# A hybrid encoder block: the last quarter of w_out in another order of token tiles, the first MLP stage in a written order, the second on shared tags

## The chip, the cores and the metric

The kernel runs on one core of one Trainium2 chip. The metric is the device time of one execution, in microseconds (us). Engines are named as the profile names them: PE is TensorE (matmuls), PEld its weight loads, DVE is VectorE, ACT is ScalarE, POOL is GpSimd, SP is the engine that issues most DMAs. ACT and POOL issue some DMAs too.

## The reference

One layer, one batch of 1024 tokens, model width 1024. Names as in the kernel:

```
h = RMSNorm(x)
[z | xBC | dt | q | k | v] = h @ W_in                 # 1024 -> 5664
ssd = gated norm of a bidirectional chunked scan (16 heads, 8 chunks of 128 tokens)
na  = neighbourhood attention on a 16 x 64 token grid, 16 heads of 64,
      QK-RMSNorm, window 8 x 16, relative-position bias
x = x + concat([ssd, na]) @ W_out                     # 2048 -> 1024
h = RMSNorm(x)
x = x + relu(h @ W1)^2 @ W2                           # 1024 -> 4096 -> 1024
```

Everything is float32. The kernel gets that accuracy out of matmuls on a rounded type: each operand is split into a high half (a rounded copy, made by ACT) and a low half (the rest, a subtraction by DVE or POOL), and a product takes three matmuls, high x high, high x low and low x high.

## The kernel before, in words

**Order of work.** After the input norm and the convolution (until 172 us in the trace) come the z, q, k, v pieces of W_in together with the scan (172 to 618), then the attention together with the first three quarters of w_out (618 to 892), the last quarter with the norm and the transposes for the MLP (892 to 974), the first MLP stage (first products from 942, alone from 975 to 1269) and the second (1272 to 1584).

**The planner.** From the pieces of W_in to the end of w_out the order of instructions on each engine comes from `Plan`: each task has an engine, an assumed cost in us, buffers that it reads and writes, and a due time; `order()` picks at each step the task that can start first (in steps of 0.35 us), the more urgent one where they tie. `run` emits the tasks in that order, inside `in_order()`, which ties each new instruction to the one before it on the same engine, so the framework's own scheduler can't move them. What is emitted outside `in_order()` the framework's scheduler orders by its own estimate of time.

**Attention.** Heads go in eight pairs; `due` puts a block of a head every 2.15 us, eight blocks a head. q and k lie in DRAM (`q_dr`, `k_dr`) as high and low halves, 64 rows for each head. `pair_loads` (L408 on) brings a pair: a q tile whose partitions 0 to 63 hold the high rows of one head and 64 to 127 the low rows (in the other order for the other head), with four DMAs of 256 KB; a k tile with the high rows in both halves, two DMAs of 512 KB for both heads at once; a tile `kl` with the low rows of k in one half and zeros in the other, two DMAs of 256 KB; and v, one DMA of 1024 KB. The scores are then two matmuls, q by k and q by kl (L1401, L1402). A w_out weight tile is loaded (L500), its high half made by ACT (L507), its low half by POOL (L510).

**The last quarter of w_out.** `groups` (L1772) is the order of 16 products, each a token tile t of 128 tokens by a half h of the columns, 12 matmuls. When both halves of a tile are added to x (`x2`, L1785), the tile is stored (`x2st`), squared and summed (L1791), its inverse root made by POOL in two instructions (`root`, L1794, L1795; the plan assumes 0.8 us), and it is normed by DVE (L1798), in place or, for tiles in `XB`, in a buffer `xn`.

**Seven products.** Both MLP stages multiply 2 x 2 blocks with seven products instead of eight (Winograd's form of Strassen's method), so sums and differences of blocks are needed: `difference` (L1770) makes those of the token tiles t and t+4, `turned` (L1758, L1762, L1763) transposes the results on PE and splits them into the operands `h1` to `h7`. Operands 1 and 2 need only tiles 0 to 3, operand 3 tiles 4 to 7, the others a pair (t, t+4). `ORD` = (1, 2, 6, 5, 7, 3, 4) is the order of the products. Products 1, 6, 7 and 4 collect in one set of PSUM tiles (X), 2 and then 5 and 3 in another (Y). So that PE has work while the last tiles are normed, three products of the first MLP stage are tasks of the plan: products 1 and 2 of block 0 and product 1 of block 1 (`block_product`).

**First MLP stage.** Eight blocks of 512 columns of W1 (`Block`). A product is 24 matmuls. `split` makes the weight operand, where needed from sums (`s1`, `s2`, L1583 to L1587), high half on ACT, low half on POOL (L369, L370); `sums` drains PSUM: copies on ACT (L1628), adds on DVE (L1633), relu and square on ACT (L1638, L1639), and the sums that are the operands of the second stage (L1646, L1648, L1650, L1654), stored to `act_dr` by SP (by POOL for the last block). In each block a product's split is emitted right ahead of the product, and the framework's scheduler places both.

**Second MLP stage.** Four parts, each with seven products of 48 matmuls; both operands are loaded and split anew: activations `ar` with ACT and DVE (`a_split`), weights with ACT and POOL, and weight differences on DVE (L1915, L1916, L1918, L1920). The results are added by DVE (L1945) to `acc`, which starts as x, loaded from DRAM (L1927), and is written out after the last part. This stage opens new SBUF pools and a new PSUM pool of its own, and is ordered by the framework's scheduler.

Of the kernel before, what the change touches and what calls it, by code (L numbers as in the profile page):

```python
# [10 lines left out]
F32 = mybir.dt.float32  # L11
# [219 lines left out]
def hymba_block(  # L231
# [64 lines left out]
    q_dr = dr.tile([2, 2, 4, P, T], F32, name="q_dr")  # L296
# [113 lines left out]
    def pair_loads(plan, p, after=()):  # L410
# [4 lines left out]
        qp = {(j, a): part(q) for j in range(2) for a in range(2)}  # L415
        kp = [part(k) for _ in range(2)]
        for j in range(2):
            for a in range(2):
                load_task(
                plan,  # L420
                    256,
                    partial(lambda j, a: q.t[a * HD : (a + 1) * HD, j].bitcast(F32), j, a),
                    partial(lambda j, a: q_dr[p // 4, a ^ j, p % 4, j * HD : (j + 1) * HD], j, a),
                    reads=after, writes=[qp[j, a]],
                    name="q",
                    since=-10.0 if p == 1 else -1e3,
                )
            load_task(
                plan,
                512,  # L430
                partial(lambda j: k.t[j * HD : (j + 1) * HD].bitcast(F32), j),
                partial(lambda j: k_dr[p // 4, 0, p % 4].rearrange("(h d) t -> d h t", h=2), j),
                reads=after, writes=[kp[j]],
                name="k",
                **free,
            )
        if p < 2:
            kls[p] = Buf(f"kl{i}"), []
            for j in range(2):
                half_, whole = part(kls[p][0]), kls[p][0]  # L440
                kls[p][1].append(half_)
                task("POOL", 1.0, partial(lambda j, b: nc.gpsimd.memset(b.t[HD * (1 - j) : HD * (2 - j), j].bitcast(F32), 0.0), j, whole), writes=[half_], name="kl0", **free)
        kl, klp = kls[i]
        for j in range(2):
            hp = slice(HD * j, HD * j + HD)
            load_task(plan, 256, partial(lambda hp, j: kl.t[hp, j].bitcast(F32), hp, j), partial(lambda hp: k_dr[p // 4, 1, p % 4, hp], hp), reads=after, writes=[klp[j]], name="kl", **free)
# [11 lines left out]
    def handed_on(plan, loaded):  # L458
# [3 lines left out]
        qp = {(j, a): part(q) for j in range(2) for a in range(2)}  # L462
# [58 lines left out]
    with ExitStack() as ph:  # L521
# [375 lines left out]
        def piece(j, b):  # L897
# [28 lines left out]
            to, w = (q_dr, 80) if kind(j) == "q" else (k_dr, 81)  # L926
# [6 lines left out]
            def turn():  # L933
                for i in range(4):
# [10 lines left out]
                    to[g, :, :, :, s].rearrange("a p f t -> f (a p) t"),  # L945
# [242 lines left out]
        def in_order():  # L1188
# [4 lines left out]
            for ins in traced[start:]:  # L1193
# [352 lines left out]
    with ExitStack() as ph:  # L1546
# [283 lines left out]
        for fb in range(8):  # L1830
# [3 lines left out]
            for i in ORD:  # L1834
                if i not in kb.w:
                    kb.split(i)
# [158 lines left out]
```

## Time and profile before

| | |
|---|---|
| median of 3 executions | 1585.77 us (1585.5 to 1588.29) |
| the profiled execution | 1589.21 us, of which its span is 1587.4 us |
| mean granted clock of PE | 0.992 |
| DVE, ACT, POOL busy | 1013.5, 720.9, 730.3 us (64%, 45%, 46% of the span) |
| DMA | 278.73 MB, 176 GB/s over the span |

The profile is of one execution. A row of its windows is: the stretch from:to in us, its length, then for PE, PEld, DVE, ACT and POOL the busy time with the number of instructions in brackets, then PE's granted clock (1.00 is full), the mean busy share of the 16 DMA engines, and GB/s. An instruction that lies in two windows counts in both. A row of the waits is: engine, tile and line that waited, what ended the wait, then us in total, times, longest. A row of the groups is: line, engine, operation, tiles, form, count, busy us, mean ns of one, idle time ahead of them and what ended it. A row of the timeline: start, us taken, what; of the chain: start, us, what; of the DMA issues: tiles, queue, count, KB each, median us from issue to landing. Matmuls overlap in the pipeline: one of 512 columns is recorded with some 0.39 us, while the next starts much sooner.

### The profile page before, as it was taken

The page shows a single profiled execution, that of the slowest core. Times are in us where ns is not written, and L with a number is a line of the kernel's source. Part 1 is how long each engine was busy: PE and PEld are TensorE (multiplying, and loading weights), DVE is VectorE, ACT ScalarE, POOL GpSimd, SP SyncE. Part 2 cuts the span into 40 slices and gives each one's busy share as a digit, 9 for nine tenths or more (in the row PEclk, how much of TensorE's full clock was granted, in tenths as well). Part 3 has the DMA queues.
Part 4 walks back from the last instruction along what each step waited for, and adds up shares of the span by engine and source line. Part 5 has one row for each costly group of instructions (what it writes and reads, how often), then busy time and mean ns, then how long its engine had stood idle before and what let it go on. Part 6 is the DMA issues. An engine that isn't in the chain of part 4 may idle for free. (4 is left out here: it accounts for less than half of the span.)

```text
span 1587.4 us, 20805 instructions
## 1 busy us (share of the span) xinstructions
PE 1548.1 (98%) x7462; PEld 1291.3 (81%) x7462; DVE 1013.5 (64%) x1414; ACT 720.9 (45%) x1187; POOL 730.3 (46%) x530
## 2 busy tenths in 40 slices
PE   7999999999999999999999998999999999999999
PEld 5788878888878888788888886888888778888887
DVE  3776444687688854567776475444444579787863
ACT  5444323444345435567686244554454444333330
POOL 2000066774779832233364353444444555555450
PEclk9999999999999999999999999999999989999999
DMA  8212398777777795978792422444443486443332
GB/s 225 54 40 70 89 311 262 231 238 248 230 209 214 225 278 172 257 208 227 193 238 94 159 94 93 174 158 146 151 155 120 159 306 251 159 161 131 107 106 80
DMA packets 184226, 278.73 MB, mean 176 GB/s; under 512 B 14819, under 2 KB 106043, under 8 KB 184123
## 3 DMA queue, kind: packets, MB, share of 16 engines
q1 hardware_dynamic: 133323, 233.88, 48.2%
q10 hardware_dynamic: 49792, 39.85, 7.6%
q0 software_dynamic: 1008, 3.67, 0.6%
q8 instruction: 59, 0.97, 0.3%
q14 instruction: 44, 0.36, 0.1%
HBM read 191.51 MB, written 89.18 MB: 177 GB/s over the span
## 5 line engine op out<-in xcount | busy, mean ns | idle before, releaser
L370 POOL TENSOR_TENSOR wl<-wraw,wh 128x1024 fp32r<-128x1024 f32 x113 | 308.7, 2743 | 305.5 <-ACT wh L369 305.5
L364 PE MATMUL pq<-wh,hTh 128*128 128x512 f32 x512 | 204.9, 400 | 2.3 <-DVE qn L931 1.7
L366 PE MATMUL pq<-wh,hTl 128*128 128x512 f32 x512 | 199.9, 390 | 0.0
L365 PE MATMUL pq<-wl,hTh 128*128 128x512 f32 x512 | 199.7, 390 | 0.1
L369 ACT ACTIVATE wh<-wraw 128x1024 fp32r<-128x1024 f32 x125 | 131.4, 1055 | 143.5 <-PE px L1221 40.1
L1221 PE MATMUL px<-wh,ahl 128*128 128x512 f32 x512 | 163.1, 395 | 4.6 <-ACT ahl L369 3.1
L1221 PE MATMUL px<-h,wh 128*128 128x512 f32 x512 | 160.1, 394 | 2.7 <-DVE cq L1633 2.7
L370 DVE TENSOR_TENSOR ahl<-ar,ahl 128x1024 fp32r<-128x1024 f32 x56 | 117.0, 2094 | 22.4 <-ACT ahl L369 21.5
L369 ACT ACTIVATE ahl<-ar 128x1024 fp32r<-128x1024 f32 x56 | 58.5, 1052 | 160.3 <-PE px L1221 80.6
L1221 PEld LDWEIGHTS px<-wh,ahl 128*128 128x128 f32 x512 | 97.6, 191 | 26.7 <-ACT ahl L369 3.6
L1221 PEld LDWEIGHTS px<-h,wh 128*128 128x128 f32 x512 | 96.6, 190 | 22.9 <-DVE cq L1633 3.1
L364 PEld LDWEIGHTS pq<-wh,hTh 128*128 128x128 f32 x512 | 96.2, 188 | 21.8 <-DVE qn L931 2.1
L366 PEld LDWEIGHTS pq<-wh,hTl 128*128 128x128 f32 x512 | 96.1, 188 | 20.8
L365 PEld LDWEIGHTS pq<-wl,hTh 128*128 128x128 f32 x512 | 96.3, 188 | 18.9 <-DVE wl L884 0.5
L1221 PE MATMUL px<-wl,ahl 128*128 128x512 f32 x256 | 101.3, 396 | 0.0
L1221 PE MATMUL px<-h,wl 128*128 128x512 f32 x256 | 100.4, 392 | 0.0
L1439 DVE TENSOR_TENSOR ptl<-ptp,pth 128x384 fp32r<-128x384 f32 (+1 forms) x128 | 65.4, 520 | 37.5 <-ACT pth L1441 36.5
L1405 DVE CUSTOM_DVE_ANT_0 pr<-psc,mb 128x384 f32<-128x384 f32 (+1 forms) x128 | 65.7, 520 | 26.6 <-PE psc L1402 23.5
L1417 ACT ACTIVATE pr<-pr,nmx 128x384 f32<-128x384 f32 (+1 forms) x128 | 74.6, 584 | 17.3 <-DVE nmx L1405 16.8
L1221 PE MATMUL pz<-h,wh 128*128 128x512 f32 x256 | 80.3, 395 | 0.8 <-DVE h L1763 0.8
L364 PE MATMUL po<-wh,yh 128*128 128x512 f32 x192 | 80.1, 417 | 0.2 <-DVE x L1327 0.2
L1221 PE MATMUL pz<-wh,ahl 128*128 128x512 f32 x256 | 80.1, 389 | 0.0
(332 smaller groups left out, 3743.4 us busy)
## 6 DMA issues: line engine op xcount, KB each, us to landing
ar<-act_dr SPq DMA_DIRECT2D x56, 512.0 KB, 4.4
act_dr<-cq SPq DMA_DIRECT2D x49, 512.0 KB, 3.0
wraw<-in_w_in_dram SPq DMA_DIRECT2D x44, 512.0 KB, 6.3
rb<-cum_dr SPq DMA_DIRECT2D x32, 512.0 KB, 6.1
wraw<-in_w_mlp_in_dram SPq DMA_DIRECT2D x32, 512.0 KB, 5.2
wraw<-in_w_mlp_out_dram SPq DMA_DIRECT2D x32, 512.0 KB, 5.6
q_dr<-hl ACTq DMA_DIRECT2D x16, 512.0 KB, 5.6
k_dr<-hl ACTq DMA_DIRECT2D x16, 512.0 KB, 3.6
```

What stands on the lines that cost most here:

```text
L364: nc.tensor.matmul(pt, lhsT=ah, rhs=bh, start=first, stop=False)
L365: nc.tensor.matmul(pt, lhsT=ah, rhs=bl, start=False, stop=False)
L366: return nc.tensor.matmul(pt, lhsT=al, rhs=bh, start=False, stop=last)
L369: nc.scalar.activation(hl[0], src, AF.Copy)
L370: eng.tensor_tensor(hl[1], src, hl[0].bitcast(F32), op=sub)
L1221: nc.tensor.matmul(pt, lhsT=a, rhs=b, start=f, stop=l, skip_group_check=True)
L1405: nc.vector.tensor_tensor_reduce(pr.t[:, 0:n], pt.t[:, 0:n], mb.t[:, o : o + n], scale=-1.0, scalar=3.0e38, op0=add, op1=ALU.min, accum_ou ...
L1417: nc.scalar.activation(pr.t[:, 0:n], pr.t[:, 0:n], AF.Exp, bias=nmx.t[:, b : b + 1], scale=-1.0, accum_out=den.t[:, hh, b : b + 1],)
L1439: nc.vector.tensor_tensor(lo[0], pv3, hi.bitcast(F32), op=sub)
```

## The change

1. **Rows of q and k.** `q_dr` changes its layout so that the high and low row of a feature lie next to each other, and the q tile holds them in alternating partitions: one DMA of 512 KB for each head over 128 partitions. k's high rows go to even and odd partitions, in four DMAs of 256 KB, each for one head; k's low rows to the even partitions. `kl` is zeroed whole. A head's scores now wait for that head's k only.
2. **Last quarter of w_out.** Another order of `groups`; tiles 3, 6 and 7 are normed into `xn` (5, 6 and 7 before); other due times; the root is planned with 1.2 us.
3. **First splits planned.** The sums of the weights of block 0 and the splits of its products 6 and 5 become tasks of the plan.
4. **First MLP stage in a written order.** Inside `in_order(skip=free_order)`, which leaves only SP to the scheduler, each step emits the split of the product after next, then its product, then its sums. Block 1 takes product 5 ahead of 6.
5. **Second MLP stage.** Its buffers are now tags of the first stage's pools (operand tiles h1 to h4 and h7, the b0 tiles that held operands 5 and 6, the weight rings, hq), and it keeps the same PSUM pool. `acc` is four tiles, two of them in the place of operand 4. The first loads and splits of part 0 are written between the products of block 7, and from there on each product of the second stage carries, between its four token tiles, the changes and splits for the product after next. All of that is in the written order.

```diff
-    q_dr = dr.tile([2, 2, 4, P, T], F32, name="q_dr")
+    q_dr = dr.tile([2, P, 2, 4, T], F32, name="q_dr")
...
+                partial(lambda j: q.t[:, j].bitcast(F32), j),
+                partial(lambda rows: q_dr[p // 4, rows, :, p % 4].rearrange("d a t -> (d a) t"), rows),
...
+            for a in range(2):
+                load_task(
+                    plan,
+                    256,
+                    partial(lambda j, a: k.t[a:P:2, j].bitcast(F32), j, a),
+                    partial(lambda rows: k_dr[p // 4, 0, p % 4, rows], rows),
+                    reads=after,
+                    writes=[kp[j]],
...
-                task("PE", 2 * (n / 2400 + 0.014), scores, reads=[qp[hh, 0], qp[hh, 1], *kp, klp[hh]], writes=[pt], due=due(b), name="psc")
+                task("PE", 2 * (n / 2400 + 0.014), scores, reads=[qp[hh], kp[hh], klp[hh]], writes=[pt], due=due(b), name="psc")
...
-        XB = [Buf("xn") if t > 4 else None for t in range(NT)]
+        XB = [Buf("xn") if t in (3, 6, 7) else None for t in range(NT)]
...
-        groups = [(0, 0), (1, 0), (2, 0), (0, 1), (1, 1), (2, 1), (4, 0), (4, 1)]
-        groups += [(3, 0), (3, 1), (5, 0), (5, 1), (6, 0), (6, 1), (7, 0), (7, 1)]
+        groups = [(0, 0), (4, 0), (1, 0), (0, 1), (4, 1), (1, 1)]
+        groups += [(t, h) for t in (5, 2, 6, 3, 7) for h in range(2)]
...
-            task("POOL", 0.8, root, reads=[ss], writes=[r0], name="r0")
+            task("POOL", 1.2, root, reads=[ss], writes=[r0], name="r0")
...
+            task("DVE", 1.23, partial(change, o, p, q, op), reads=read, writes=[b], since=52.0, name="mlps")
+        w6 = split_task(s2, Buf("w"), "POOL", due=68.0)
+        w5 = split_task(s1, Buf("w"), "POOL", due=74.0)
...
+        made = [(0, 1), (0, 2), (1, 1)]
+        row = [(fb, i) for fb in range(8) for i in ((1, 2, 5, 6, 7, 3, 4) if fb == 1 else ORD)]
+        left = [m for m in row if m not in made]
+        for fb, i in row[:49]:
+            kb = blocks[fb]
+            if i == 1:
+                kb.load("12", "21", "22")
+                kb.tiles()
+            with in_order(skip=free_order):
+                if (fb, i) in made:
+                    kb.to = kb.Y if i == 2 else kb.X
+                else:
+                    split_of(*left[left.index((fb, i)) + 2])
+                    kb.product(i)
+                kb.sums(i)
...
+        rings = {
+            "ahl": [over(hA, f"h{i}{n}") for i in (1, 2, 3) for n in range(2)],
+            "hl": [over(b0, t) for t in ("k", "v", "kl")] + [of_wp] * 3,
+            "raw": [over(arp, "wraw", F32), over(hq, "q", F32)],
+            "ar": [over(arp, "ar", F32), over(b0, "q", F32)],
+            "t": [over(hA, f"h7{n}", F32) for n in range(2)],
+        }
...
+            def ready(self, i, change=True):
+                for u in range(2):
+                    if change:
+                        self.change(i, u)
+                    yield
+                self.split_a(i)
+                yield
+                for u in range(2):
+                    self.split_w(i, u)
+                yield
...
+            kb.split(7)
+            kb.product(6)
+            o.split_a(1)
+            kb.sums(6)
+            o.load_a(2)
+            kb.split(3)
+            kb.product(5)
+            o.split_w(1, 0)
+            kb.sums(5)
+            o.load("12")
+            o.load("22")
+            kb.split(4)
+            kb.product(7)
+            o.split_w(1, 1)
+            o.split_w(2, 0)
+            kb.sums(7)
+            kb.product(3)
+            o.split_a(2)
+            o.split_w(2, 1)
+            kb.sums(3)
+            kb.product(4)
+            o.change(6, 0)
+            o.change(6, 1)
+            kb.sums(4)
+            load_acc(0)
+            row = [(o, i) for i in ORD] + [(p, i) for p in map(Part, range(1, 4)) for i in ORD]
+            for n, (o, i) in enumerate(row):
+                ahead = iter(row[n + 2][0].ready(row[n + 2][1], n > 0) if n + 2 < len(row) else ())
+                for _ in o.product(i):
+                    next(ahead, None)
+                if n == 1:
+                    begun = load_acc(1)
```

Here `split_w`, `split_a` and `change` are the weight split (ACT and POOL), the activation split (ACT and DVE) and the weight differences (DVE) of one product of part `o` of the second stage.

More of the change, by code (lines that the diff above doesn't have):

```diff
@@ L414, in pair_loads @@
         q, k, v = Buf(f"q{i}"), Buf(f"k{i}"), Buf(f"v{i}")
-        qp = {(j, a): part(q) for j in range(2) for a in range(2)}
-        kp = [part(k) for _ in range(2)]
+        qp, kp = ([part(b) for _ in range(2)] for b in (q, k))
         for j in range(2):
[L418 to L427, printed above, removed]
+            rows = slice(j * HD, (j + 1) * HD)
             load_task(
@@ L925, in piece @@
             qn, sq, rq, tp = Buf("qn"), Buf("sq"), Buf("rq"), Buf("tp")
-            to, w = (q_dr, 80) if kind(j) == "q" else (k_dr, 81)
+            w = 80 if kind(j) == "q" else 81
             col = pcol[:, w : w + 1]
@@ L1580, in split @@
                     self.load("12", "21", "22")
-                if i == 6:
+                if i in (5, 6) and "s1" not in a:
                     a["s1"], a["s2"] = raw_tile(), raw_tile()
@@ L1829, in hymba_block @@
         hq = ph.enter_context(tc.tile_pool(name="hq", bufs=1, reuse_waits="tile"))
-        for fb in range(8):
-            kb = (k0, k1)[fb] if fb < 2 else Block(fb)
-            kb.load("12", "21", "22")
-            kb.tiles()
-            for i in ORD:
-                if i not in kb.w:
-                    kb.split(i)
-                if not (i == 1 and fb < 2 or i == 2 and fb == 0):
-                    kb.product(i)
-                elif i == 1:
-                    kb.to = kb.X
-                else:
-                    kb.to = kb.Y
-                kb.sums(i)
@@ L1949, in hymba_block, with load_acc @@
                         )
+                    yield
+        def load_acc(h):
+            for n in range(2):
+                acc[2 * h + n] = t = over(*((hA, f"h4{n}"), (hq, "q"))[h], F32)("acc")
+                for m in range(2):
+                    last_ = nc.sync.dma_start(t[:, m], x2_dr[4 * h + 2 * n + m])
+            return last_
+        kb, o = blocks[7], Part(0)
+        kb.load("12", "21", "22")
+        kb.tiles()
+        o.load("11")
+        o.load_a(1)
+        o.load("21")
+        with in_order(skip=free_order):
+            kb.split(6)
+            kb.product(1)
+            kb.sums(1)
+            kb.split(5)
+            kb.product(2)
+            kb.sums(2)
+            kb.split(7)
[30 more added lines that the diff above has]
+                    begun = load_acc(1)
+                    tc_after = begun.ins
+                if i == 5 and o.fb < 3:
+                    row[n + 4][0].load_all(tc_after if o.fb == 0 else None)
+    b0s.close()
     arps.close()
```

225 lines of the change are left out of this document (119 added, 106 removed).

## The prediction

> **What bounds the kernel.** I read the page first, then the chain of waits that ended last, then TensorE's own waits.
>
> ```profile
> PE 1548.1 (98%) x7462; PEld 1291.3 (81%) x7462; DVE 1013.5 (64%) x1414; ACT 720.9 (45%) x1187; POOL 730.3 (46%) x530
> ```
>
> ```profile
> 1325.33 8.01 PE px L1221 x34
> 1333.33 10.88 PE pz L1221 x48
> ...
> 1572.69 10.89 PE px L1221 x48
> ```
>
> TensorE is busy 98% of the span of 1587.4 us, and the chain is TensorE alone from 1325 us on: 48 matmuls in 10.88 us, 0.2267 us each, without a hole. No edit changes the number or the shape of a matmul, so the change can only fill holes, and the page leaves 1587.4 - 1548.1 = 39 us of them, more where the clock was low. TensorE's waits say where they lie:
>
> ```profile
> PE po L365 <- POOL wl L510: 3.9, 2, 3.2
> PE pv L1369 <- ACT pth L1441: 3.3, 1, 3.3
> ...
> PE px L1221 <- DVE cq L1633: 2.7, 1, 2.7
> PE ptn L1758 <- POOL x L1770: 2.5, 1, 2.5
> PE ptn L1758 <- DVE h L1763: 2.3, 3, 1.3
> ```
>
> Three places: `po` and `pv` are the attention with the w_out quarters in it; `ptn` is the end of w_out's last quarter, with the norm and the transposes; `px` is the seam between the two MLP stages. The change touches all three.
>
> **Seam of the MLP stages.** The windows by 5 us:
>
> ```profile
> 1255.00:1260.00 5.00, 5.00 (x24) 4.14 (x23) 5.00 (x3) 1.06 (x1) 5.00 (x3) 1.00 0.69 257
> 1260.00:1265.00 5.00, 2.31 (x11) 1.61 (x10) 5.00 (x4) 0.20 (x1) 1.95 (x1) 1.00 0.00 0
> 1265.00:1270.00 5.00, 4.43 (x12) 3.14 (x12) 0.96 (x2) 5.00 (x6) 2.92 (x2) 0.66 0.01 3
> 1270.00:1275.00 5.00, 2.45 (x6) 1.97 (x7) 4.81 (x3) 5.00 (x7) 3.30 (x3) 0.68 0.90 311
> 1275.00:1280.00 5.00, 4.17 (x11) 2.77 (x10) 5.00 (x3) 3.18 (x4) 4.12 (x4) 0.50 0.99 378
> 1280.00:1285.00 5.00, 5.00 (x19) 3.99 (x18) 5.00 (x4) 0.00 (x0) 3.71 (x3) 0.80 1.03 415
> ```
>
> A full window shows 24 matmuls (first row). The next five show 59 instead of 120: 61 x 0.2267 = 13.8 us lost, part of it in waiting, part in the clock of 0.50 to 0.80 that follows the waiting. VectorE is full at the start of it, with this:
>
> ```profile
> 1259.62 3.42 DVE L1916 TENSOR_TENSOR wraw<-wraw 128x1024 f32<-128x1024 f32 x1
> 1262.96 1.21 DVE L1918 TENSOR_TENSOR wraw<-wraw 128x1024 f32<-128x1024 f32 x1
> 1264.09 0.67 DVE L1633 TENSOR_TENSOR cq<-cq,px 128x512 f32<-128x512 f32 x1
> ```
>
> Differences of the second stage's weights (L1916, L1918) stand ahead of the add (L1633) that frees the PSUM tile of block 7, and product 4 waits for that tile. The new code writes the order out: the add comes before the second stage's work, and product 1's operands are split during products 6, 5 and 7 of block 7. The cover, engine by engine, a product of block 7 being 24 x 0.2267 = 5.44 us:
>
> POOL, at 2.5 us a split (row L370 below), has at most three in one product (7.5 us) and then one in the next, 10 us in 10.9; it also issues block 7's seven stores, which the new splits are moved past:
>
> ```profile
> 1269.22 0.57 POOL L1619 DMA_DIRECT2D act_dr<-cq  x1
> ```
>
> 0.6 us each, 4 us in five products, so it still ends ahead of product 1. VectorE has, after product 3, three sums, four weight differences and the last sum, 8 x 1.21 = 9.7 us behind 2.8 us of relu and square (priced below), and reaches product 1's first add 7 us after that product began. That holds the adds to `acc`, not TensorE: product 1's PSUM is wanted again by product 6, 2 x 10.88 = 21.8 us after product 1 began. The new wait is that of the `acc` loads: their buffers are now operand 4's, so they can issue only when product 4 has read it. Queued behind them on SP are the next activation loads, on VectorE everything behind the first add. Four loads of 512 KB take 5 to 7 us at the 311 to 415 GB/s of the windows, inside the 21.8; uncovered they would cost those 5 to 7. In all -13.8, less 1.0 for a first product that starts ragged: **-12.8** (bounds -13.8 and -7). Within the second stage every operand is written two products ahead, and the chain has no hole there now: 0.
>
> **Last quarter of w_out.** First its last `po` matmul, then the windows behind it:
>
> ```profile
> 941.50 0.39 PE L366 MATMUL po<-wside,kl 128*128 128x512 f32 x1
> ```
>
> ```profile
> 950.00:975.00 25.00, 19.36 (x104) 15.25 (x103) 19.60 (x23) 11.15 (x19) 11.06 (x6) 0.93 0.15 46
> ```
>
> ```profile
> 975.00:980.00 5.00, 5.00 (x17) 3.90 (x15) 1.37 (x3) 2.21 (x4) 0.00 (x0) 0.68 0.87 297
> ```
>
> Idle 25 - 19.36 = 5.6; clock 0.07 x 19.36 + 0.32 x 5 = 3.0: 8.6 us. Tile t+4 is subtracted from tile t, and only then can four of the seven operands be transposed. Before, the pairs (0,4), (1,5), (2,6), (3,7) completed at steps four, six, seven and eight; now at two, four, six and eight, so one pair's differences are left at the end where two were bunched. That last chain (add, square, root, norm, four differences, transposes) has the three planned products as cover, 3 x 5.44 = 16.3 us. Against it: tile 3 is now seventh instead of fifth. It is multiplied one step (24 matmuls, 5.4 us) ahead of the last, and its own add, square, root, norm and transposes take longer than that, so operands 1 and 2, which the planned products read, can come after the last `po`; and three weight differences with two POOL splits are planned into a stretch where VectorE is busy 19.60 of 25. Bounds: -8.6, all hidden, and +2.7, half a step bare. I take **-5.5**, nearer the first, since TensorE's waits in this stretch are for differences (L1770) and what follows them.
>
> **Attention.** Rows of q and k are interleaved: a q load now fills 128 partitions where it filled 64, in two DMAs a pair instead of four, and k comes in four of 256 KB instead of two of 512. Bytes are the same. The windows, ScalarE's longest wait for a DMA, and the loads:
>
> ```profile
> 665.00:670.00 5.00, 4.49 (x25) 3.71 (x23) 2.96 (x9) 1.00 (x4) 2.07 (x3) 1.00 1.07 368
> 670.00:675.00 5.00, 1.78 (x7) 1.21 (x7) 0.00 (x0) 0.00 (x0) 2.61 (x2) 1.00 1.03 239
> 675.00:680.00 5.00, 2.15 (x8) 1.76 (x9) 2.24 (x5) 3.74 (x10) 2.37 (x1) 0.79 0.60 171
> ```
>
> ```profile
> ACT wh L507 <- DMA wraw<-in_w_out_dram: 10.3, 1, 10.3
> ```
>
> ```profile
> v<-v_dr SPq DMA_DIRECT2D x8, 1024.0 KB, 7.3
> q<-q_dr SPq DMA_DIRECT2D x32, 256.0 KB, 9.1
> k<-k_dr SPq DMA_DIRECT2D x16, 512.0 KB, 8.6
> ```
>
> One hole of 0.51 + 3.22 + 2.85 us, with 0.21 x 2.15 in the clock: 7.0 us. ScalarE stood 10.3 us for a w_out weight while the DMA engines were full (share 1.03 to 1.07). A q load has a quarter of v's bytes and lands later. If q, k and kl held the engines for less time, that weight would land sooner; but the planner gets other tasks and orders the whole stage anew. Bounds: -7.0, and +7.0 for one such hole elsewhere. I take **-3.0**, nearer to the q and v rows than to the reshuffle.
> [...]
>
> **First MLP stage in a written order.** Here nothing can be won:
>
> ```profile
> 1000.00:1025.00 25.00, 25.00 (x112) 20.72 (x111) 11.51 (x10) 12.50 (x17) 12.17 (x5) 1.00 0.52 189
> ```
>
> Splits are written two products ahead; the tightest is that of product 6 of the next block. VectorE, POOL and ScalarE from 1000 to 1250 us:
>
> ```profile
> L1650 DVE TENSOR_TENSOR cq<-cq 128x1024 f32<-128x1024 f32 x7 | 21.8, 3108 | 0.0
> ...
> L1633 DVE TENSOR_TENSOR cq<-cq,py 128x512 f32<-128x512 f32 x14 | 9.6, 685 | 24.9 <-ACT cq L1628 14.7 <-PE py L1221 10.2
> ...
> L1648 DVE TENSOR_TENSOR cq<-cq 128x1024 f32<-128x1024 f32 x7 | 8.5, 1215 | 0.0
> ```
>
> ```profile
> L370 POOL TENSOR_TENSOR wl<-wraw,wh 128x1024 fp32r<-128x1024 f32 x47 | 117.3, 2496 | 137.2 <-ACT wh L369 137.2
> ```
>
> ```profile
> L369 ACT ACTIVATE wh<-wraw 128x1024 fp32r<-128x1024 f32 x47 | 49.9, 1062 | 90.8 <-issue 30.1 <-PE pz L1221 25.5 <-PE px L1221 23.7
> ```
>
> After product 3: add, relu and square, 0.7 + 2 x 1.06 = 2.8; six VectorE sums in a row (three of product 3, one of product 4, two for the weight), 6 x 1.22 = 7.3; one POOL split in front of one of them, 2.5; then 1.06 and 2.5 for the split of product 6 itself: 16.2 us. Product 6 starts three products later, 16.3 us, and needs the low half at its third matmul, 0.45 on. Half a us of slack, with hand-overs between engines not counted, at six block changes: **+1.0**. Bounds 0 and +12, if one more POOL split comes in front and each block change is 2.0 us late.
> [...]
>
> **Sum.** -12.8 - 5.5 - 3.0 + 1.0 = -20.3. The profiled execution took 1589.2 (its span and 1.8 around it), so 1568.9; it lies 3.4 above the median of 1585.77, on whose scale that is **1565.5**.
>
> **Rivals.**
> A, the forecast: 1565.5, by its own unknowns 1558 to 1572. 0.60.
> B, the slow loads were the whole cause in the attention: -7.0 in place of -3.0, 1561.5. For it the q and v rows; against it that a weight also waits for a free buffer. 0.13.
> C, the new tile order doesn't do what it says: the last pair's chain ends as late as before, since tile 3 comes late and VectorE is nearly full. 5.5 back, 1571. 0.11.
> D, product 6 is late at each block change: 12 back, 1577.5; at 3 us each 18 back, 1583.5. For it the half us of slack; against it that POOL has one split to put in front, not two. 0.08.
> E, slower: two k loads now write alternate rows of one half tile. If the second is held until the first has landed, 8.6 to 9.1 us come twice in a row. Place: the start of each of the seven pairs loaded in the attention; price: that of the measured hole, 7.0 us. From three late pairs on (21 us) the gain is gone; at five it is 1565.5 + 35 = 1600. Against it: the plan gives a pair 16 x 2.15 = 34 us, and the next is loaded meanwhile. 0.08.
>
> **How the numbers follow.** A measurement of this kernel can tell about 0.2%, 3.2 us, from no change: 1582.6 to 1588.9 is the same. Faster: A, B, C and half of D, 0.88. Same: the other half of D, and E at three pairs, 0.06. Slower: the rest of E, 0.06. At its best the last quarter gives 3.1 more, the attention 4.0, the block changes 1.0 and the seam 1.0: 1556.4, the low end. The high end takes in C, and D at 12: 1580. Left out are E and the far half of D, 0.12.
>
> **What would show it.** Right: 24 matmuls in every 5 us through the seam at a clock of 1.00; under 4 us lost between the last `po` and the first stage's steady run; no ScalarE wait near 10 us for w_out, and q loads landing well under 9.1 us. Wrong: TensorE waiting for `wl` L370 at every block change, 38 us apart (D); for q or k at pair starts (E); or for the adds to `acc` at product 6 of the second stage.

## The result and the profile after

| | before | after |
|---|---|---|
| median | 1585.63 us (1583.2 to 1588.29, 4 runs) | 1559.13 us (1557.95 to 1562.73, 4 runs) |
| profiled execution | 1589.21 us, span 1587.4 | 1558.86 us, span 1557.1 |
| mean granted clock of PE | 0.992 | 1.000 |

The ratio is 0.9836, 95% interval 0.9814 to 0.9859: 26.5 us or 1.6% faster. The page after, first row:

```profile
PE 1535.2 (99%) x7462; PEld 1284.3 (82%) x7462; DVE 1000.1 (64%) x1414; ACT 725.8 (47%) x1187; POOL 709.6 (46%) x530
```

The same 7462 matmuls; TensorE's idle time went from 39 to 1557.1 - 1535.2 = 22 us.

**Seam.** Windows after, where block 7 ends and the second stage begins:

```profile
1240.00:1245.00 5.00, 5.00 (x24) 4.14 (x23) 3.68 (x2) 3.18 (x4) 5.00 (x3) 1.00 0.38 108
1245.00:1250.00 5.00, 5.00 (x24) 4.14 (x23) 2.78 (x4) 2.67 (x4) 3.31 (x2) 1.00 0.77 268
1250.00:1255.00 5.00, 5.00 (x24) 4.14 (x23) 4.93 (x5) 3.39 (x4) 2.16 (x4) 1.00 0.99 338
1255.00:1260.00 5.00, 5.00 (x24) 4.14 (x23) 4.97 (x6) 3.07 (x4) 0.66 (x2) 1.00 1.04 385
```

24 matmuls in each at full clock: the hole is gone. VectorE after, from its timeline, has the add (L1639) 15 us ahead of the differences (L1942), which stood in front of it before:

```profile
1237.45 0.69 DVE L1639 TENSOR_TENSOR cq<-cq,px 128x512 f32<-128x512 f32 x1 [2.04 <-PE px L1227]
1241.32 4.75 DVE L370 TENSOR_TENSOR ahl<-ar,ahl 128x1024 fp32r<-128x1024 f32 x2 [3.17 <-ACT ahl L369]
...
1253.02 1.22 DVE L1942 TENSOR_TENSOR wt<-wraw 128x1024 f32<-128x1024 f32 x1
```

**Last quarter of w_out.** Windows after, and TensorE's waits from 920 to 1000 us:

```profile
925.00:950.00 25.00, 22.50 (x129) 18.68 (x128) 22.91 (x29) 13.38 (x23) 13.65 (x9) 1.00 0.23 85
950.00:975.00 25.00, 25.00 (x120) 20.88 (x119) 7.51 (x12) 11.44 (x16) 9.58 (x4) 1.00 0.40 127
975.00:1000.00 25.00, 23.87 (x106) 19.43 (x105) 14.93 (x13) 15.21 (x18) 10.59 (x4) 1.00 0.51 188
```

```profile
PE px L1227 <- DVE h L1769: 2.5, 1, 2.5
PE pz L1227 <- POOL wl L370: 1.1, 1, 1.1
```

The waits for `ptn` have gone, and the clock stays at 1.00. Two holes remain, 2.5 us idle before the first product of the MLP and 1.1 us where block 0 passes into block 1.

**Attention.** The window of the hole, before and then after, and three kinds of load after:

```profile
665.00:690.00 25.00, 18.42 (x97) 15.77 (x96) 12.11 (x33) 10.78 (x30) 11.95 (x10) 0.93 0.89 245
```

```profile
665.00:690.00 25.00, 25.00 (x154) 22.43 (x153) 18.58 (x52) 17.25 (x46) 9.78 (x10) 1.00 0.85 285
```

```profile
k<-k_dr SPq DMA_DIRECT2D x32, 256.0 KB, 6.5
q<-q_dr SPq DMA_DIRECT2D x16, 512.0 KB, 6.2
wraw<-in_w_out_dram SPq DMA_DIRECT2D x16, 512.0 KB, 6.7
```

The hole is not there, a q load of twice the size lands in 6.2 us instead of 9.1, and ScalarE no longer waits for a w_out weight.

To compare stages, I use the time that TensorE lost in them, from each run's one trace: over the stage's matmuls, what each spacing from start to start exceeds the usual spacing of the same two shapes in that trace, summed; a low clock counts in it. The tail is the last quarter of w_out with what follows it up to 1000 us, the seam the place where the second MLP stage begins. All runs of this study:

| kernel | median us | span us | attention 600-900 | w_out tail 900-1000 | second stage from 1225 |
|---|---|---|---|---|---|
| before | 1585.6 | 1587.4 | 28.4 | 12.3 | 13.6 |
| place_only | 1580.1 | 1579.5 | 19.6 | 11.5 | 13.4 |
| rows_only | 1579.3 | 1578.3 | 18.5 | 11.7 | 14.2 |
| diffs_later | 1582.8 | 1587.9 | 29.8 | 11.2 | 12.4 |
| no_rows | 1568.0 | 1560.4 | 20.0 | 7.7 | -0.1 |
| old_tiles | 1559.5 | 1556.9 | 18.5 | 6.8 | -0.1 |
| old_dues | 1567.7 | 1565.8 | 18.4 | 14.2 | -0.2 |
| old_tiles_dues | 1565.4 | 1562.7 | 18.7 | 12.3 | -0.2 |
| old_turns | 1563.4 | 1562.4 | 18.4 | 11.2 | -0.2 |
| splits_after | 1567.9 | 1565.0 | 18.4 | 13.6 | -0.2 |
| no_order | 1564.7 | 1562.9 | 18.4 | 6.9 | 5.5 |
| plain_seam | 1567.3 | 1564.9 | 18.5 | 6.3 | 6.3 |
| mended | 1556.9 | 1555.3 | 18.4 | 3.4 | -0.2 |
| after | 1559.1 | 1557.1 | 18.4 | 6.4 | -0.1 |

From 1000 to 1225 us all lie between -0.4 and -0.2. Before to after, the three stages give 10.0 + 5.9 + 13.7 = 29.6 of the 30.3 us of span. The medians come from four occasions, on which before took between 1583.76 and 1585.63 us; after was timed on one of them, so a difference of 2 us from after is not told from none by the medians alone. Of old_dues and of splits_after one execution each took about 4 ms (3995.7 and 3992.43 us); nothing here says why, and without them the medians would be 0.1 and 0.9 us lower.

### The profile page after: what moved, and what is told of

The parts are those of the page before. It is cut to its first block, busy times and chain, and to the rows that moved or that the text cites. A ratio compares the mean times of both kernels' runs of the same rounds, so it can differ in the third digit from the quotient of the medians.

```text
span 1557.1 us, 20808 instructions
## 1 busy us (share of the span) xinstructions
PE 1535.2 (99%) x7462; PEld 1284.3 (82%) x7462; DVE 1000.1 (64%) x1414; ACT 725.8 (47%) x1187; POOL 709.6 (46%) x530
## 3 DMA queue, kind: packets, MB, share of 16 engines
q1 hardware_dynamic: 133323, 233.88, 47.0%
## 4 chain that ended last, share of the span: by engine, by line
PE 91%; issue 3%; POOL 2%; DVE 2%; DMA 1%; ACT 1%; SPq 1%; ACTq 0%; POOLq 0%; DVEq 0%
PE px L1227 22%; PE pz L1227 11%; PE pq L364 6%; PE pq L365 6%; PE pq L366 6%; PE py L1227 5%; PE po L364 3%; PE po L365 3%; PE po L366 3%; PE pv L1375 3%; PE px L366 3%; PE px L365 3%; PE px L364 3%; PE ptp L1435 2%; PE pd L1132 2%
## 5 line engine op out<-in xcount | busy, mean ns | idle before, releaser
L370 POOL TENSOR_TENSOR wl<-wraw,wh 128x1024 fp32r<-128x1024 f32 x74 | 184.1, 2496 | 199.8 <-ACT wh L369 196.6
L369 ACT ACTIVATE wh<-wraw 128x1024 fp32r<-128x1024 f32 x86 | 90.3, 1057 | 84.3 <-DVE wraw L1590 30.8
L370 DVE TENSOR_TENSOR ahl<-ar,ahl 128x1024 fp32r<-128x1024 f32 x56 | 108.5, 1978 | 7.3 <-ACT ahl L369 7.3
L369 ACT ACTIVATE ahl<-ar 128x1024 fp32r<-128x1024 f32 x56 | 58.0, 1056 | 95.7 <-DMA ar<-act_dr 33.5
L1227 PE MATMUL px<-whl,ahl 128*128 128x512 f32 x408 | 96.5, 389 | 0.0
L1227 PEld LDWEIGHTS px<-whl,ahl 128*128 128x128 f32 x408 | 76.6, 188 | 15.9
L370 POOL TENSOR_TENSOR whl<-wraw,whl 128x1024 fp32r<-128x1024 f32 x21 | 57.8, 2763 | 63.1 <-ACT whl L369 62.9
L1227 PE MATMUL px<-wh,ahl 128*128 128x512 f32 x240 | 77.9, 390 | 0.0
```

The source lines that it names most:

```text
L369: nc.scalar.activation(hl[0], src, AF.Copy)
L370: eng.tensor_tensor(hl[1], src, hl[0].bitcast(F32), op=sub)
L1227: nc.tensor.matmul(pt, lhsT=a, rhs=b, start=f, stop=l, skip_group_check=True)
```

## Experiments

**place_only**: the kernel before, in which only the partitions that q, k and kl are loaded into change; tasks, sizes and bytes of the loads stay. (The high and low rows of q are placed to match, and `kl` is zeroed whole.)

```diff
-                    partial(lambda j, a: q.t[a * HD : (a + 1) * HD, j].bitcast(F32), j, a),
+                    partial(lambda j, a: q.t[a:P:2, j].bitcast(F32), j, a),
...
-                partial(lambda j: k.t[j * HD : (j + 1) * HD].bitcast(F32), j),
+                partial(lambda j: k.t[j:P:2].bitcast(F32), j),
...
-            load_task(plan, 256, partial(lambda hp, j: kl.t[hp, j].bitcast(F32), hp, j), partial(lambda hp: k_dr[p // 4, 1, p % 4, hp], hp), reads=after, writes=[klp[j]], name="kl", **free)
+            load_task(plan, 256, partial(lambda hp, j: kl.t[0:P:2, j].bitcast(F32), hp, j), partial(lambda hp: k_dr[p // 4, 1, p % 4, hp], hp), reads=after, writes=[klp[j]], name="kl", **free)
```

> The kernel before with nothing but the partitions changed into which q, k and kl are loaded: every other partition of 128 instead of 64 adjacent ones. DRAM layout, number and size of the DMAs, the plan's tasks, costs and dependencies stay as they were, so the planned order stays too. Theory T (a load into 64 adjacent partitions holds the DMA engines longer for its bytes, and this alone made the attention's hole): 7 to 10 us less than before, no hole between 665 and 685 us, q landing in about 6 us instead of 9.1, and a DMA share under 0.95 in the windows from 640 to 690 us. Rival R (the new plan of the attention moved the hole, the speed of the loads does not matter): within 1.5 us of before, the hole stays, q lands in about 9 us.

Measured: 1580.07 us against 1584.93 for before on the same chip, ratio 0.9971 (0.9958 to 0.9983): -4.9 us. Its loads, and then the row of the w_out weights before:

```profile
q<-q_dr SPq DMA_DIRECT2D x32, 256.0 KB, 5.0
k<-k_dr SPq DMA_DIRECT2D x16, 512.0 KB, 5.4
wraw<-in_w_out_dram SPq DMA_DIRECT2D x16, 512.0 KB, 7.1
```

```profile
wraw<-in_w_out_dram SPq DMA_DIRECT2D x16, 512.0 KB, 9.8
```

The same 32 loads of 256 KB land in 5.0 us instead of 9.1 when their 64 partitions are every other one instead of adjacent; the w_out weights behind them in 7.1 instead of 9.8. The window of the hole, which here lies 5 us sooner, is full:

```profile
660.00:685.00 25.00, 25.00 (x151) 22.37 (x150) 17.84 (x48) 16.89 (x46) 12.06 (x10) 1.00 0.83 285
```

So the partitions make the gain, not the plan: TensorE and VectorE have the same instructions in the same order as before. Theory T asked for 7 to 10 us; the two profiled executions lie 8.0 apart (1589.21 and 1581.25), the medians only 4.9. The DMA share is not under 0.95 throughout either: two of the ten windows from 640 to 690 us have 1.06 and 0.98. Why it matters which partitions are written, no run shows. What is shown beside the landing times: on q1, where these loads lie with others, the same 133323 packets with 233.88 MB took 46.1% of the time of 16 engines over the span, and 48.2% before.

**rows_only**: before with the whole of the change's part 1 (q in two loads of 512 KB, k in four of 256 KB, a score waiting for its own head's k).

```diff
-    q_dr = dr.tile([2, 2, 4, P, T], F32, name="q_dr")
+    q_dr = dr.tile([2, P, 2, 4, T], F32, name="q_dr")
...
-        qp = {(j, a): part(q) for j in range(2) for a in range(2)}
-        kp = [part(k) for _ in range(2)]
+        qp, kp = ([part(b) for _ in range(2)] for b in (q, k))
...
```

> The kernel before with the whole first part of the change alone (interleaved q and k rows, one q DMA a head over 128 partitions, k in four DMAs, scores that wait for one head's k). Theory T: 8 to 10 us less than before, the same as with the partitions alone to within 1.5 us, since the plan adds nothing. Rival R: also 8 to 10 us less, but then 7 us or more beyond the run with the partitions alone.

Measured: 1579.34 us, ratio 0.9963 (0.9949 to 0.9978): -5.6 us, within 1 us of place_only and, like it, less than the 8 to 10 us of theory T. That the planner orders the stage anew costs and gains nothing that shows in the medians; in the lost time it is 1.1 us (19.6 to 18.5).

**no_rows**: after, with part 1 undone (the same diff backwards).

> The kernel after with the first part of the change undone (q and k as before), everything else as after. Theory that the parts add: 8 to 10 us slower than after, about 1568, 17 to 19 us less than before, and a hole of TensorE of 5 us or more between 660 and 690 us. Rival (the parts help each other, or the hole had gone elsewhere): within 3 us of after.

Measured: 1567.99 us, 8.9 above after, as forecast. Yet its profiled execution, 1562.22, the fastest of its four (to 1570.85), has no hole in the attention, though its q loads land in 9.9 us:

```profile
q<-q_dr SPq DMA_DIRECT2D x32, 256.0 KB, 9.9
k<-k_dr SPq DMA_DIRECT2D x16, 512.0 KB, 8.7
```

The profile of diffs_later, below, is of the slowest of its ten executions (1589.71; the fastest took 1579.55), and has the hole again, at 670 us. Up to 900 us TensorE, VectorE and SP have the same instructions in the same order in before, in diffs_later and in no_rows. So with the slow loads the hole comes in some executions and not in others: the slow loads make it possible, and what brings it in the one and not in the other stays open. Three profiles suggest that this is most of the spread of before; it was not counted.

**old_tiles**: after, with the old order of token tiles and the old `xn` buffers.

```diff
-        groups = [(0, 0), (4, 0), (1, 0), (0, 1), (4, 1), (1, 1)]
-        groups += [(t, h) for t in (5, 2, 6, 3, 7) for h in range(2)]
+        groups = [(0, 0), (1, 0), (2, 0), (0, 1), (1, 1), (2, 1), (4, 0), (4, 1)]
+        groups += [(3, 0), (3, 1), (5, 0), (5, 1), (6, 0), (6, 1), (7, 0), (7, 1)]
```

> The kernel after with the old order of token tiles in the last quarter of w_out (and tiles 5, 6, 7 normed into the side buffer again); due times, the root's planned cost and the planned splits stay new. Theory (the order in which pairs complete was the cause): 4 to 7 us slower than after, with TensorE waiting for differences and transposes between 940 and 975 us. Rival (due times, costs and planned splits did it): within 1.5 us of after. Second rival (tile 3 coming earlier fills the start of the planned products better): 2 to 3 us less than after, its 2.8 us wait of product 1 for its operand gone.

Measured: 1559.51 us (1558.63 to 1560.38), ratio to before 0.9836 (0.9816 to 0.9856): the same as after. The tile order is worth nothing here, and my argument from the steps at which pairs complete falls. Tile 3 comes earlier, and the hole before the first product of the MLP shrinks, from 2.76 to 0.92 us, but TensorE waits 1.4 us for `ptn` in its place.

**old_dues**: after, with the due times and the root's cost of before in the last quarter.

```diff
-            load(512, partial(lambda t: x2_dr[t], t), partial(lambda xt: xt, xt), reads=X2[t], due=at + 6, late=-5.0, name="x2st")
+            load(512, partial(lambda t: x2_dr[t], t), partial(lambda xt: xt, xt), reads=X2[t], due=at + 12, name="x2st")
...
-            task("POOL", 1.2, root, reads=[ss], writes=[r0], name="r0")
+            task("POOL", 0.8, root, reads=[ss], writes=[r0], name="r0")
-            late = 46 + 3.0 * u if u < 3 else at + 12
+            late = 58 + 1.5 * u if u < 3 else at + 14
...
```

> The kernel after with the planner's old due times and the old cost of the root in the last w_out quarter (x2 stores at +12, transposes of operands 3, 4 and 5 to 7 at their old times, the root at 0.8 us); tile order, planned splits and written order as after. Theory D (due times and costs shortened the tail): the loss between 900 and 1000 us rises from 6.3 to 10 to 12 us, the time by 4 to 6 us. Theory W (the block's splits being planned, so that none slips into the last pair's chain, shortened it): within 1.5 us of after.

Measured: 1567.7 us, 8.6 above after; the loss in the tail is 14.2 us. TensorE's waits from 920 to 1000 us:

```profile
PE px L1227 <- DVE h L1769: 2.2, 1, 2.2
PE ptn L1764 <- DVE h L1769: 1.8, 2, 1.0
PE ptn L1764 <- DVE xn L1804: 1.5, 1, 1.5
PE px L1227 <- ACT cq L1634: 1.2, 1, 1.2
```

The waits for `ptn` are back as in the kernel before: transposes wait for VectorE to drain their PSUM tile (L1769), and for the last norm (L1804). Theory D holds, and its price is more than forecast (10 to 12 us in the tail, 4 to 6 in all).

**old_tiles_dues**: both of these.

> The kernel after with both the old order of token tiles and the old due times and root cost in the last w_out quarter; first-block splits still planned, MLP stages in the written order. Apart, old tiles cost nothing and old due times 8 us. Theory D (the new due times shorten the tail whatever the tile order): 1565 to 1568, a loss of 11 us or more between 900 and 1000 us. Rival F (due times have only to fit the tile order; old with old is as good as new with new): 1558.5 to 1561, a loss under 8 us there.

Measured: 1565.35 us, 12.3 us lost in the tail. Theory D again: the new due times save some 6 us with the old tile order (1565.35 - 1559.51 = 5.8) and 8 with the new. They are no fitting of one to the other. The 12.3 us are those of before, though here the splits are planned and the MLP stages written out: with the old due times these save the tail little. (Of the 12.3 here 1.29 lie at a change of blocks, which is treated below, and none before.)

**old_turns**: the old due times for the transposes alone.

> The kernel after with the old due times of the transposes alone (operands 3, 4 and 5 to 7); the x2 stores' due time and the root's cost as in after. Theory D1 (the transposes' due times carry the 8 us that the old due times cost: due only at 58 us and later, they are put behind the three planned products' matmuls, and product 6 waits for them): 1565 to 1568. Rival D2 (the x2 stores, 6 us earlier and ahead of the weights on SP's queue, and the root's cost carry it): within 1.5 us of after's 1559.1.

Measured: 1563.43 us (1562.28 to 1565.07), 4.3 above after, half of what all the old due times cost. Neither theory alone: the transposes carry one half, and by the difference the stores of x2 and the root's cost carry the other; these two were not told apart.

**splits_after**: after, with block 0's differences and splits of operands 6 and 5 behind the plan instead of in it.

```diff
...
-        w6 = split_task(s2, Buf("w"), "POOL", due=68.0)
-        w5 = split_task(s1, Buf("w"), "POOL", due=74.0)
...
+        with in_order(skip=free_order):
+            k0.split(6)
+            k0.split(5)
```

> The kernel after, but the first block's three weight differences and its splits of operands 6 and 5 are not planned into the w_out quarter: they stand, in that order, right behind its last instruction. VectorE ends the last transposes at 957.9 us; three differences of 1.23, a rounding on ScalarE of 1.06 and a remainder on POOL of 2.4 then end at 965.0, where TensorE wants operand 6 at 958.3. Theory W (that planning them, with the tail kept free of unplanned work, is what the tail gained): product 6 starts 6.7 us late, and 2 to 3 us of reduced clock follow as they did behind the hole of the kernel before; the time rises by 6 to 10 us. Theory D (due times alone): the loss moves to product 6 but the pairs' chain ends earlier by what left it, and the time rises by less than 3 us.

Measured: 1567.89 us, some 8 above after, 13.6 us lost in the tail. TensorE's wait and ScalarE's timeline:

```profile
PE px L1227 <- ACT cq L1634: 3.7, 1, 3.7
```

```profile
961.77 2.00 ACT L369 ACTIVATE wh<-wraw 128x1024 fp32r<-128x1024 f32 x2 [3.26 <-DVE wraw L1590]
963.68 1.05 ACT L1634 COPY cq<-px 128x512 f32<-128x512 f32 x2
```

As theory W forecast, though not by its route: TensorE lost 3.9 us at once and 1.8 more with the clock behind it (granted 0.93 from 950 to 975 us), and what it waited for last was not operand 6 but the PSUM tile that product 6 adds to. The copy that reads product 1 out of it (L1634) stands behind the two roundings (L369) on ScalarE, and those wait for the differences. A wait that names a copy can have its cause in the instruction ahead of the copy. Some 1.5 us of the loss are not product 6's: the hole of 2.76 us before the first product, as long as in after, was followed here by a granted clock of 0.71 from 935 to 940 us, and in after by 1.00 (from 925 to 950 us: 0.93, and 1.00 in after). And the kernel before has these splits neither planned nor behind the plan in a written order, but placed by the scheduler, so the 8 us are not what planning them gained.

**diffs_later**: before, with the second stage's first differences on VectorE held behind the add that product 4 waits for.

```diff
-                        nc.vector.tensor_tensor(c, c, pt, op=add)
+                        summed = nc.vector.tensor_tensor(c, c, pt, op=add)
+                        if i == 7:
+                            self.add7 = summed
...
+                    with ExitStack() as later:
+                        if fb == 0:
+                            later.enter_context(tc.issue_after(kb.add7.ins))
...
```

> The kernel before with one edit: the weight differences of the second MLP stage's first quarter (L1915, L1916, L1918) may issue on VectorE only behind block 7's second px add of product 7 (L1633), as in the written order of the kernel after; pools, tags and loads are untouched. Theory S1 (the seam's hole begins because those differences stand ahead of the add): the 5.8 us in which TensorE waited for L1633 (3.1 + 2.7) go, product 4 follows product 3 without a gap, and what is left of the hole, some 8 of 13.6 us, lies before product 1 of the second stage, which waits for its operands; the time falls by 3 to 6 us. Rival S2 (the hole is made by the second stage's late buffers, and the differences only fill it): TensorE reaches product 1 earlier and waits there so much longer; the time stays within 1 us.

Measured: 1582.79 us, ratio 0.9988 (0.997 to 1.0006). Its waits in the seam, and then TensorE's for the same operand before:

```profile
ACT ahl L369 <- DMA ar<-act_dr: 13.8, 3, 10.6
...
PEld px L1221 <- ACT ahl L369: 6.7, 1, 6.7
PE px L1221 <- ACT ahl L369: 6.2, 1, 6.2
```

```profile
PE px L1221 <- ACT ahl L369: 3.1, 1, 3.1
```

The wait for the add is gone, and product 1 waits so much longer for its activation operand. (The rows of PEld and PE are one wait seen twice; my expectation added them, and the wait for the add was 2.7 to 3.1 us, not 5.8.) The hole has a second cause right behind the first, so taking away the first alone gains nothing that the medians show. (By the traces the seam lost 9.2 us instead of 13.1, since less low clock followed, 0.88, 0.50 and 0.93 in three windows of 5 us where before had 0.66, 0.68, 0.50 and 0.80 in four, and 2.8 of these went again at 1321 us, where TensorE waited for the low half of an activation.) ScalarE's timeline says what holds the operand:

```profile
1266.45 1.06 ACT L369 ACTIVATE wh<-wraw 128x1024 fp32r<-128x1024 f32 x1 [3.65 <-DVE wraw L1921]
...
1271.60 1.99 ACT L369 ACTIVATE ahl<-ar 128x1024 fp32r<-128x1024 f32 x2
```

Roundings of the differences stand ahead of the activation's (`ahl`) there too.

**no_order**: after, with all engines left to the scheduler in the MLP stages.

```diff
-        free_order = (mybir.EngineType.SP,)
+        free_order = (mybir.EngineType.SP, mybir.EngineType.PE, mybir.EngineType.Activation, mybir.EngineType.DVE, mybir.EngineType.Pool)
```

> The kernel after, its shared tags, planned splits and statement order kept, but nothing in the two MLP stages is tied to the written order, so the framework's scheduler orders the instructions of every engine there. Theory S1 (order makes the seam): the scheduler puts the second stage's differences (L1942, L1943, L1945) between and ahead of block 7's px and pz adds again, TensorE waits for them, and 6 to 14 us of the hole come back. Rival S2 (shared tags and early buffers make it): no hole at the seam, the time stays. For the tail of the last w_out quarter: theory W (the written order keeps the first block's weight work out of the last pair's chain) expects one weight difference (L1593) to slip in among the transposes, 1.2 us on VectorE, and 1 to 5 us more lost between 900 and 1000 us; theory D (due times) expects no change there.

Measured: 1564.66 us (1564.12 to 1564.69), 5.5 above after. The second stage lost 5.5 us, but not at the seam:

```profile
1265.00:1270.00 5.00, 5.00 (x24) 4.14 (x23) 5.00 (x4) 1.20 (x2) 3.71 (x4) 1.00 1.04 349
1270.00:1275.00 5.00, 5.00 (x24) 4.14 (x23) 5.00 (x1) 2.71 (x3) 5.00 (x3) 1.00 0.88 336
...
1310.00:1315.00 5.00, 4.23 (x19) 3.19 (x17) 5.00 (x4) 0.00 (x0) 1.92 (x1) 1.00 0.00 0
1315.00:1320.00 5.00, 3.98 (x18) 3.32 (x19) 5.00 (x8) 0.54 (x1) 0.00 (x0) 1.00 0.62 207
```

```profile
PE px L1227 <- DVE acc L1993: 4.6, 5, 2.0
```

In the order of its instructions, differences do stand between block 7's adds, VectorE is full in every window, and the seam stays closed: 0.4 us lost. The loss comes from 1313 us on, at the adds to `acc`, which VectorE no longer finishes in time. S1 falls for the seam, S2 holds there; what the written order is worth is 5.5 us in the second stage. One difference did slip among the last transposes (W), and cost 0.5 us in the tail.

**plain_seam**: as no_order, and the second stage's first loads, splits and differences written behind block 7 instead of among its products.

```diff
-            o.split_a(1)
             kb.sums(6)
-            o.load_a(2)
...
             kb.sums(4)
+            o.load("11")
+            o.load_a(1)
+            o.load("21")
+            o.load_a(2)
...
```

> The kernel after with its shared tags and buffers, nothing in the MLP stages tied to the written order, and the second stage's first loads, splits and differences written behind block 7's last product (as in the kernel before) instead of among its products; the framework's scheduler may still pull them forward. Theory S2 (the shared tags alone make the seam close, since loads and splits find free buffers early): as with the written statements but no ties, 1564.7 within 1.5 us, and under 3 us lost between 1240 and 1320 us. Rival S3 (the place of the statements makes it): loads and splits of the second stage come late again, and 5 to 11 us of the 13.6 come back, 1569 to 1575.

Measured: 1567.34 us (1564.18 to 1568.22), between the two forecasts; by its trace 6.3 us are lost, 3.5 of them between 1240 and 1320 us, where S2 allowed 3, and most of the rest at 1329 us, at an add to `acc`. That is nearer to S2. So of the 13.7 us of the seam, 5.5 (by the medians: 13.7 - 8.2) to 7.3 (by the lost time: 13.6 - 6.3) come without the written order and without the place of those statements. What is left of the change there is the shared tags and the one PSUM pool. With them the second stage's loads start early, as SP's timeline shows: before, then plain_seam, then after:

```profile
1241.37 8.10 SPq L1898 DMA_DIRECT2D wraw<-in_w_mlp_out_dram  x6
1253.78 0.82 SPq L1873 DMA_DIRECT2D ar<-act_dr  x2
```

```profile
1224.61 0.42 SPq L1925 DMA_DIRECT2D ar<-act_dr  x1
1226.50 0.38 SPq L1915 DMA_DIRECT2D wraw<-in_w_mlp_out_dram  x1
```

```profile
1218.14 5.15 SPq L1915 DMA_DIRECT2D wraw<-in_w_mlp_out_dram  x2
1226.50 0.87 SPq L1925 DMA_DIRECT2D ar<-act_dr  x2
```

In plain_seam the first weights of the second stage are asked for at 1204.04 us, and the row shows the second of its first two activation loads. Product 1 of the second stage begins at 1248.07 us after: its activations are asked for 21.6 us ahead. Before it was due at 1267.4 (product 4 at 1262, which takes 5.44 us), 13.6 ahead of that. SBUF tags and PSUM pool were not told apart.

**mended**: a try at a faster kernel, at the two holes that remain.

```diff
...
-            w = split_task(raw, Buf("w"), "POOL")
+            w = split_task(raw, Buf("w"), "POOL", since=53.4 if kb.fb == 1 else -1e3)
...
                     kb.product(i)
+                if (fb, i) == (0, 3):
+                    split_of(1, 5)
                 kb.sums(i)
```

> The kernel after with its two remaining holes between 925 and 1000 us taken up. First: the remainder split (L1705) for block 1's product 1 stands on POOL behind the last pair's POOL difference instead of ahead of it, so that the DVE difference of tile 3, 2.85 us beside that split, should take the 0.69 us of its like; the hole of 2.76 us before product 1 shrinks to 0.6. Second: the three weight differences of block 1 (L1589 to L1591) stand ahead of product 3's sums of block 0, not behind them; the 1.29 us before the second pz goes. Theory P (the differences are late because POOL's wide operation holds VectorE up, and the block change is late by the chain of sums and differences): 3 to 4 us under after's 1559.1, 1555 to 1556. Rival (the product waits anyway, for tile 3's transposes, which come behind the last but one step of w_out): the first hole stays over 2 us, the total gains 1.3 at most.

Measured: 1556.88 us (1555.24 to 1557.13), ratio to before 0.9818 (0.9803 to 0.9832); after has 0.9836 (0.9814 to 0.9859), so the intervals overlap, while the spans differ by 1.8 us and the lost time by 3.0. VectorE and POOL after:

```profile
932.95 2.85 DVE L1776 TENSOR_TENSOR xn<-xn,x 128x512 f32<-128x512 f32 x1 [0.18 <-POOL wl L1705]
```

```profile
929.55 5.71 POOL L1705 TENSOR_TENSOR wl<-wraw,wh 128x1024 fp32r<-128x1024 f32 x2
```

And in mended, first VectorE and then POOL:

```profile
934.14 0.69 DVE L1776 TENSOR_TENSOR xn<-xn,x 128x512 f32<-128x512 f32 x1 [0.18 <-POOL wl L1705]
```

```profile
936.15 2.40 POOL L1705 TENSOR_TENSOR wl<-wraw,wh 128x1024 fp32r<-128x1024 f32 x1
```

The same difference takes 2.85 us beside POOL's second remainder split and 0.69 where that split comes later. The hole before the first product went from 2.76 to 0.60 us, though a new one of 0.84 opened at 939 us, and that at the block change went from 1.29 to nothing. Theory P's mechanism holds, with 2.3 us by the medians where it asked for 3 to 4; by its median it is the fastest kernel of the study.

## Why the prediction was right, and where it was wrong

The forecast was 1565.5 us in a range from 1556 to 1580; 1559.13 lies inside, 6.4 below the forecast. On the scale of the profiled execution, 1568.9 was forecast and 1558.86 came. By steps:

- **Seam, -12.8: -13.7.** The size is right; 24 matmuls in 5 us came as said, and no ragged first product. The cause is right by half. "Differences ... stand ahead of the add" is what the trace shows, but taking that away alone gave 1.2 us of the lost time and nothing in the medians (diffs_later). The step that failed is "The new code writes the order out" as the whole reason: the shared buffers alone bring 5.5 to 7.3 us, the place of the statements 0.8 to 2.7, and the written order 5.5. Even these 5.5 are not taken from the hole: without the written order nearly all of them are lost from 1313 us on, where the kernel before lost about 1 us. The `acc` loads cost TensorE nothing, as forecast.
- **Last quarter, -5.5: -5.9**, and -7.2 without the 1.29 us of the block change that lie in the same stretch. The right size from a wrong step, so by luck. "One pair's differences are left at the end where two were bunched" is worth nothing (old_tiles); besides, the first pair is complete in the third step, not the second. What the runs show in its place is the due times (with the root's planned cost): from old_tiles_dues to old_tiles, which differ in nothing else, the tail's loss falls from 12.3 to 6.8 us. I had listed the planned splits as a burden on VectorE; moved behind the plan they cost some 8 us (splits_after), but no run places them as the kernel before did, so their share of the gain is not shown. The step against, "operands 1 and 2 ... can come after the last `po`", did happen, with 2.76 us as bounded by 2.7. Two things go into it: tile 3 late, and a POOL split planned beside its difference; without the first it was 0.92 us (old_tiles), without the second 0.60 (mended).
- **Attention, -3.0: -10.0 in the profiled executions, -4.9 to -5.6 by the medians on before and -8.9 on after.** The mis-sized term. The loads made the gain (place_only), so rival B's condition held as far as the runs tell, and I weighed the planner's reshuffle too high: it is some 1 us, and a gain. And the hole cost 28.4 - 20.0 = 8.4 us with the low clock behind it, 0.79 and 0.87 in the two windows from 675 to 685 us (before against no_rows, which has slow loads and no hole), where I had 7.0.
- **The 3.4 us from the profiled execution to the median.** I carried it over. But, as far as the profiles tell, it belonged to the hole, which not every execution has; after, the profiled execution lies 0.3 us from the median. So the errors, 7.0 in the attention, 0.9 in the seam, 1.4 in tail and block changes together, and 0.7 elsewhere, come to 10.0, and the wrong carry takes 3.7 back. That the median came out only 6.4 below the forecast is in part luck.
- **First stage, +1.0: 1.29 us once, 0 at the other six changes.** At these six the chain that I worked out is the one: in one of them product 3 ends at 1014.15 us and the low half of product 6 is ready at 1030.27, 16.1 us where I had 16.2, and in all six it comes 0.65 to 0.80 us ahead of its need. But no run shows the 2.5 us that I counted for a POOL split in front of a sum: at each of the six, after has one sum beside the split (L1654, 3.30 to 3.31 us, POOL's L370 2.49) and its like right behind it without one (L1656, 1.21), so 2.1 us more. The wait, at 991 us, is another. Product 1 of block 1 is multiplied early, by the plan, so the product that waits there (product 5) comes two products after product 3 and not three: its low half is wanted 11.3 us after product 3 and is ready after 12.6. My sum has no term for this change, so that 1.29 lies near 1.0 is luck.
- **Rivals.** C's claim, that the tile order does nothing, was true, but its price wasn't, for other parts of the change did the work. D, product 6 late at each block change, did not come. Nor did E: k in four loads lands in 6.5 us, and no wait for q or k shows.

## What to carry to other kernels

When a wait is taken away, look up what is late right behind it: here the operand was late right behind the add, and moving the add alone gained nothing that showed; with the shared buffers the loads came earlier, and most of the hole went. A size that fits does not show that its reason is right; an edit has several parts, and each must be undone alone, and the likely pairs together, before the gain is given to one of them. Before a term is scaled from one profile, ask whether the hole comes in every execution.

## What the runs showed of the hardware

Loads of 256 KB over 64 partitions landed in 5.0 us (median of 32) when every other partition was written, and in 9.1 when they were adjacent; v, 1 MB over 128, fell from 7.3 to 6.5 beside them. I had expected part of this, not that it is nearly a half. The VectorE difference of tile 3 (L1776), 0.69 us in mended, where no POOL split ran beside it, took 2.85 in after beside one; the sums of the first stage took 3.30 to 3.31 us beside a split and 1.21 without, at six block changes. What lies behind either was not shown.
